# Ten adaLN pieces summed on VectorE and closed with a column of ones, in a two-block diffusion kernel

## The chip, the cores and the metric

One core of one Trainium2 chip runs the whole program as one launch. The metric is device time in microseconds, from the start of an execution to its end; the number given is the median of several executions. The inputs and the output are fp32 in the chip's main memory.

## The reference, cut to what matters

Two blocks of two layers each work on 256 latent rows and 256 context rows of width 1024. Each layer has adaLN modulation: a condition vector `c` (for latent rows) and another, `c_ctx` (for context rows), go through silu and one wide matrix, and the result is cut into shift, scale and gate columns.

```python
mod_lat = (silu_c @ ada_w[i] + ada_b[i])[:, None, :]
mod_ctx = silu_cc @ ada_w[i] + ada_b[i]
...
m = jax.nn.silu(cond) @ w_mod + b_mod
return jnp.split(m[..., None, :], N_MOD, axis=-1)
...
    if not last:
        hcf = modulate(rms_norm(xc, norm_ffn[l]), csh2, csc2)
        xc = xc + cg2 * conv_ffn(hcf, w_up[l], conv_w[l], w_down[l])
```

In the last layer of each block the context rows need only the first shift and scale (their keys and values are still read); the gate, and in the second block the second shift, scale and gate, are used for latent rows alone. The first block's matrices are 1024 x 3072, the second block's 1024 x 6144.

## The kernel before, in words

All weights arrive by DMA as raw fp32 chunks of 128 partitions x 1024 (512 KB). ScalarE casts a chunk to a high half in the matmul's reduced type (`whi`, L180 through the recording helper), VectorE subtracts it from the raw chunk for the low half (`wlo`), and each product is made of three matmuls: high by high, high by low, low by high (`mm3`, L195 at the matmul call). A unit of the feed-forward's up-projection is one chunk and 24 matmuls of 512 columns; it is called v or g and a number (v9, g10) after the table of orders. A down-projection unit is d and a number.

Three raw buffers (`RAW`, L97) and four pairs of high and low halves (`HL`) form a ring. `weights_hi` (L347) and `weights_lo` (L363) walk over all chunks in the order of use, one after the other; a chunk that may not be prepared yet holds up all behind it. `load_chunks` (L330) issues the next load on SyncE's queue when VectorE has subtracted a chunk. `run_items` (L392) takes the units in order and issues their matmuls. Other work (evictions, norms, the scan heads, the closing steps of adaLN pieces) runs as chains that are stepped by a clock of estimates while the program is written, so that one program order comes out for each engine.

The strings `L0_ORDER` (L148), `MIX1`, `MIX2` and `FFN` (L163) give the order of units by hand; each letter A is one adaLN chunk, taken from the list `ada_left` (L717 to L722). A piece is 512 columns of an adaLN matrix, four chunks of 256 rows x 512 columns: `mod1` has pieces 0 to 5, `bmod1` pieces 0 to 11. `ada_one` (L526) makes a piece as follows: the four columns of `cond` (silu of the two condition vectors, each as high and low part, tile `condc`) are the stationary side, a chunk's halves the moving side, 16 matmuls in all into a 4 x 512 bank; then ScalarE copies the bank to `ada_r`, TensorE transposes it in four parts, ScalarE copies that to `ada_t`, and VectorE adds the parts and the bias into the tile `mod1` or `bmod1`.

In the scan layer the pieces 4 and 5 of `mod1` stand as `z7 A q8 f8 A b8 A v8 A z8 A q9 f9 A b9 A z9 A o2 o3 q10 f10 A` (the first of these is the last chunk of piece 3). In the feed-forward of the second block's first layer the pieces 4 to 10 of `bmod1` stand between v8 and d8; after v8, v9, v11 and v12 come the last chunk of one piece and the first of the next, after v10 the last two and the first, after d4 the last chunk of piece 9 and two of piece 10. The four chunks of piece 11 stand alone in the last layer.

Of the kernel before, what the change touches and what calls it, by code (L numbers as in the profile page):

```python
# [20 lines left out]
P = 128  # L21
# [60 lines left out]
def tile_two_blocks(ctx: ExitStack, tc: tile.TileContext, I, out: bass.AP):  # L82
# [19 lines left out]
    def bank(kind="mm"):  # L102
        p = ps_mm if kind == "mm" else ps_sm
        return p.tile([P, 512], F32, tag="ps" + kind, name="ps" + kind)
# [7 lines left out]
    def small(tag, n=16):  # L112
        return sp.tile([P, n], F32, tag=tag, name=tag)
# [91 lines left out]
    def spawn(gen, delay=0.0):  # L205

        chains.append([when(*delay) if isinstance(delay, tuple) else clk[0] + delay, gen, None])

    def tell(key, t=None):

        done[key] = last[0] if t is None else t
# [288 lines left out]

    cst, mod = {}, {}

    def cond_split(cname, ccname):

        st = const.tile([P, KD, 4], F32R, tag="cond" + cname, name="cond" + cname)
        for j, nm in enumerate((cname, ccname)):
            sg = small("cs_s", 8)
            act.activation(sg[:, :8], col[nm], AF.Sigmoid)
            dve.tensor_tensor(sg[:, :8], sg[:, :8], col[nm], ALU.mult)
            act.copy(st[:, :, 2 * j], sg[:, :8])  # L510
            dve.tensor_tensor(st[:, :, 2 * j + 1], sg[:, :8], st[:, :, 2 * j], ALU.subtract)
        cst[cname] = st
# [10 lines left out]

    ada_open = {}

    def ada_one(w, cname, bias, b0, mname, j, k2):  # L526
        if (mname, j) not in ada_open:
            ada_open[mname, j] = []
        hold = ada_open[mname, j]

        def fin():
            r = sp.tile([4, 512], F32, tag="ada_r", name="ada_r", bufs=1)
            act.copy(r, hold[0][:4, :])
            sm_hold(-1)
            yield
            ps = bank("sm")
            for b in range(4):
                tr(ps[:, 4 * b:4 * b + 4], r[:, b * P:(b + 1) * P], ident[:4, :4])
            t4 = sp.tile([P, 16], F32, tag="ada_t", name="ada_t", bufs=2)
            act.copy(t4, ps[:, :16])  # L540
            v = t4.rearrange("p (b v h) -> p b v h", b=4, v=2)
            m = mod[mname][:, 4 * j:4 * j + 4, :]
            dve.tensor_tensor(m, v[:, :, :, 0], v[:, :, :, 1], ALU.add)
            dve.tensor_tensor(m, m, col[bias][:, b0 + 4 * j:b0 + 4 * j + 4].unsqueeze(2).to_broadcast([P, 4, 2]),
                              ALU.add)
            tell((mname, j))

        def run(wk):
            if k2 == 0:
                yield sm_room(1)  # L550
                sm_hold(1)
                hold.append(bank("sm"))
            for i in range(2):
                k = 2 * k2 + i
                mm(hold[0][:4, :], cst[cname][:, k, :], wk[i][0], k == 0, False)
                mm(hold[0][:4, :], cst[cname][:, k, :], wk[i][1], False, k == KD - 1)
            if k2 == 3:
                spawn(fin())
            yield 0

        return Item(run, cut(w[k2 * 256:(k2 + 1) * 256, j * 512:(j + 1) * 512]))
# [17 lines left out]
        tell("g" + name)  # L579


    def mod_cols(gain, m, sc, sh, name):

        A = const.tile([P, 8, 2], F32, tag="A" + name, name="A" + name)
        dve.tensor_scalar(A, m[:, sc:sc + 8, :], 1.0, None, ALU.add)
        dve.tensor_tensor(A, A, gain.unsqueeze(2).to_broadcast([P, 8, 2]), ALU.mult)
        return A, m[:, sh:sh + 8, :]


# [212 lines left out]
    def hgrn(hd):  # L802

        l0 = st.l0
        x, qs = st.X[hd], st.q[hd]
        Kd = l0.tile([P, T], F32, tag="Km", name="Kd", bufs=2)
        dve.tensor_tensor(Kd, x[:, 0], x[:, 3], ALU.add)
# [17 lines left out]
        for lv in range(7):  # L825
            h = 1 << lv
            nb = T // (2 * h)
            ps = bank("sm")
            for c in range(4):
                mm(ps[:, c * P:(c + 1) * P], Km[:, c * P:(c + 1) * P],  # L830
                   ap_of(x, T + c * P, [[2 * h, P // (2 * h)], [T + h, 2], [1, h]]), True, True)
            t = Tl.rearrange("p d (b s) -> p d b s", s=2)
            xs = x.rearrange("p k (b s i) -> p k b s i", s=2, i=h)
            dve.tensor_tensor(xs[:, 2:4, :, 1], xs[:, 2:4, :, 1],
                              t[:, :, :, 0].unsqueeze(3).to_broadcast([P, 2, nb, h]), ALU.mult)
            dve.tensor_tensor(xs[:, 0:2, :, 0], xs[:, 0:2, :, 0],
                              t[:, :, :, 1].unsqueeze(3).to_broadcast([P, 2, nb, h]), ALU.mult)
            Tl = l0.tile([P, 2, max(nb, 8)], F32, tag=f"T{lv + 1}", name="Tn", bufs=1)[:, :, :nb]
            dve.tensor_tensor(Tl, t[:, :, :, 0], t[:, :, :, 1], ALU.mult)
            dve.copy_predicated(A.rearrange("p c t -> p (c t)"),  # L840
                                st.lvl[:, lv].rearrange("p c t -> p (c t)"), ps)
            if lv < 6:
                yield (x,)
                Km = mixed_keys(lv + 1)
            yield (x, Km)
        if hd:
            yield has(("O", hd - 1))
        ps = bank("sm")
# [156 lines left out]
    def l1_kv_chain():  # L1005
        l1 = st.l1
        kv_r = st.kv_r
        ss, rs = small("pn_ss", 4), small("pn_rs", 4)
        jk = bank("sm")
        for tk in range(4):  # L1010
            act.activation(jk[:, tk * P:(tk + 1) * P], kv_r[:, tk, 0:128], AF.Square, accum_out=ss[:, tk:tk + 1])
        rsqrt(rs[:, 0:4], ss[:, 0:4], 1.0 / 128, 4)
        dve.tensor_tensor(kv_r[:, :, 0:128], kv_r[:, :, 0:128],
                          rs[:, 0:4].unsqueeze(2).to_broadcast([P, 4, 128]), ALU.mult)
        kp = row2k("kp", (P, 4, 1, 2, 64))
        for tk in range(4):
            src = kv_r[:, tk, 128:192].unsqueeze(1)
            if tk < 2:
                for j in range(2):
                    dve.tensor_copy(kp[:, tk, :, j], src)  # L1020
            else:
                rope_mla(kp[:, tk], src, tk - 2, 1)
        yield
        ps = bank("sm")
        for tk in range(4):
            tr(ps[:, tk * P:(tk + 1) * P], kv_r[:, tk, 0:128], ident)
        tm = row2k("tm")
        dve.tensor_scalar(tm, ps, col["kvan"], None, ALU.mult)
        split(st.kvT[0], st.kvT[1], tm)
        ps = bank("sm")  # L1030
        for tk in range(4):
            tr(ps[:, tk * P:(tk + 1) * P], kp[:, tk].rearrange("p a b c -> p (a b c)"), ident)

        kh = row2k("kh", dt=F32R)
        act.copy(kh, ps)
        dve.tensor_copy(st.kst[0:64], kh[0:64])
        dve.tensor_tensor(st.kst[64:128], ps[64:128], kh[64:128], ALU.subtract)
        tm = row2k("tm2", (P, 4, 128))
        dve.tensor_tensor(tm, kv_r[:, :, 0:128], st.kvg.unsqueeze(1).to_broadcast([P, 4, 128]), ALU.mult)
        split(st.kvR[0], st.kvR[1], tm)  # L1040
        tell("kv")

    def l1_qa_chain():
        qa_r = st.qa_r
        ss, rs = small("pn_ss", 4), small("pn_rs", 4)
        jk = bank("sm")
        for tk in range(2):
            act.activation(jk[:, :256], qa_r[:, tk], AF.Square, accum_out=ss[:, tk:tk + 1])
        rsqrt(rs[:, 0:2], ss[:, 0:2], 1.0 / 256, 2)
        dve.tensor_tensor(qa_r, qa_r, rs[:, 0:2].unsqueeze(2).to_broadcast([P, 2, 256]), ALU.mult)  # L1050
        yield
        ps = bank("sm")
        for k in range(2):
            for tk in range(2):
                tr(ps[:, k * 256 + tk * P:k * 256 + (tk + 1) * P], qa_r[:, tk, k * P:(k + 1) * P], ident)
        tm = row2k("tm", (P, 2, 256))
        for k in range(2):
            dve.tensor_scalar(tm[:, k], ps[:, k * 256:(k + 1) * 256], col["qan"][:, k:k + 1], None, ALU.mult)
        split(st.qaT[0], st.qaT[1], tm)
        tell("qa")  # L1060
# [273 lines left out]
    def b2_items(l):  # L1334
# [378 lines left out]
        def ffn_norm(g):  # L1713
            yield mods(bm, 24, 40)
            if l not in st.ABf:
                st.ABf[l] = mod_cols(col["ffn"][:, 8 * l:8 * l + 8], mod[bm], 32, 24, f"f{l}")
            yield from norm_chain([xr[tk] for tk in g], lambda: st.ABf[l], 1 - g[0] // 2, hT[fk], g, fkey, ())


# [170 lines left out]
    for i in range(2):  # L1890
        for _ in load_cols(i):
            pass
    cond_split("c", "cc")
    for nm in ("mod0", "mod1"):
        mod[nm] = const.tile([P, 24, 2], F32, tag=nm, name=nm)
# [130 lines left out]
```

## Time and profile before

| | |
|---|---|
| median of 3 runs | 2336.43 us (2333.97 to 2337.26) |
| the profiled execution, its own time | 2340.02 us |
| its span, first to last instruction | 2338.0 us |
| granted TensorE clock, mean | 0.983 |
| busy: TensorE, VectorE, ScalarE | 96%, 71%, 48% of the span |
| chain that ended last | TensorE 85%, VectorE 7%, ScalarE 2%, DMA 2% |

The profile is one execution. Busy is the time in which an engine had an instruction under way; a matmul's time in it includes its way through the array, so the distance between two starts tells how long the queue is held. An idle stretch in front of an instruction is put down to what ended it.

### The profile page before, as it was taken

What the parts mean: (1) busy time and instruction counts of PE and PEld (TensorE: products, weight loads), DVE (VectorE), ACT (ScalarE), POOL (GpSimd) and SP (SyncE); (2) the same over time, 40 slices, a digit from 0 to 9 for tenths busy, and PEclk for the clock granted to TensorE, in tenths of its full rate; (3) what the DMA queues carried; (4) which work ended last, traced back from release to release, by engine and by line L of the source; (5) the groups of instructions that cost most, each with busy time, mean ns of one, the idle gap of its engine ahead of it and who ended that gap; (6) DMA issues with size and microseconds to landing.
All of it is one profiled execution on the core that took longest, in us unless ns stands there. A gap on an engine that the chain in (4) does not pass through costs nothing.

```text
span 2338.0 us, 33916 instructions
## 1 busy us (share of the span) xinstructions
PE 2237.4 (96%) x13051; PEld 1903.2 (81%) x13051; DVE 1669.5 (71%) x3016; ACT 1124.7 (48%) x1963; POOL 35.8 (2%) x38
## 2 busy tenths in 40 slices
PE   5999999999999987999899999999999999998998
PEld 3888888888888877888788878877777888997987
DVE  6677867777778777888657844688746646876976
ACT  7344444444444445556445533556523335655644
POOL 0000000000000000000000000100010010000000
PEclk8999999999999998999999999999999999999999
DMA  7223324332434233233422344277643233455664
GB/s 253 68 73 116 101 91 126 91 108 91 131 96 126 91 107 94 77 110 113 146 82 91 90 146 124 63 216 210 210 141 109 90 109 112 134 171 154 190 189 135
DMA packets 324042, 290.63 MB, mean 124 GB/s; under 512 B 10561, under 2 KB 257705, under 8 KB 323881
## 3 DMA queue, kind: packets, MB, share of 16 engines
q1 hardware_dynamic: 323881, 288.47, 40.4%
q8 instruction: 103, 1.69, 0.3%
q14 instruction: 58, 0.48, 0.1%
HBM read 287.34 MB, written 1.09 MB: 123 GB/s over the span
## 4 chain that ended last, share of the span: by engine, by line
PE 85%; DVE 7%; ACT 2%; DMA 2%; issue 1%; SPq 0%; DVEq 0%; ACTq 0%
PE psmm L195 63%; PE pssm L195 18%; PE pssm L201 3%; DVE wlo L180 2%; ACT whi L180 1%; DMA wraw<-in_w_in_dram 1%; DMA wraw<-in_w_mod_dram 0%; DVE x L180 0%; DMA wraw<-in_w_out_dram 0%; DVE rs_t L180 0%; ACT pssm L180 0%; DVE hlo L180 0%; DVE PT L180 0%; DVE nh_t L180 0%; DVE rp L180 0%
## 5 line engine op out<-in xcount | busy, mean ns | idle before, releaser
L180 DVE TENSOR_TENSOR wlo<-wraw,whi 128x1024 fp32r<-128x1024 f32 (+1 forms) x504 | 608.0, 1218 | 190.4 <-ACT whi L180 184.0
L180 ACT CAST whi<-wraw 128x1024 fp32r<-128x1024 f32 (+1 forms) x504 | 519.0, 1039 | 392.5 <-PE psmm L195 276.9
L195 PE MATMUL psmm<-hhi,whi 128*128 128x512 f32 (+1 forms) x1832 | 654.5, 357 | 5.1 <-ACT hhi L180 2.8
L195 PE MATMUL psmm<-hhi,wlo 128*128 128x512 f32 (+1 forms) x1832 | 637.6, 348 | 13.4 <-DVE wlo L180 13.4
L195 PE MATMUL psmm<-hlo,whi 128*128 128x512 f32 (+1 forms) x1832 | 636.4, 347 | 4.8 <-DVE hlo L180 4.8
L195 PEld LDWEIGHTS psmm<-hhi,wlo 128*128 128x128 f32 x1832 | 352.0, 192 | 58.6 <-DVE wlo L180 15.5
L195 PEld LDWEIGHTS psmm<-hhi,whi 128*128 128x128 f32 x1832 | 352.8, 193 | 48.9 <-ACT whi L180 3.1
L195 PEld LDWEIGHTS psmm<-hlo,whi 128*128 128x128 f32 x1832 | 352.7, 193 | 42.5 <-DVE hlo L180 5.8
L180 DVE TENSOR_TENSOR X<-X,Tn 128x512 f32<-128x512 f32 x192 | 124.0, 688 | 56.5 <-PE pssm L195 28.9
L195 PE MATMUL psmm<-whi,yh 128*128 128x512 f32 x412 | 163.7, 397 | 0.4 <-ACT yh L180 0.4
L195 PE MATMUL psmm<-wlo,yh 128*128 128x512 f32 x412 | 160.7, 390 | 0.4 <-DVE wlo L180 0.4
L195 PE MATMUL psmm<-whi,yl 128*128 128x512 f32 x412 | 160.7, 390 | 0.0
L195 PE MATMUL psmm<-whi,hhi 128*128 128x256 f32 x464 | 136.6, 294 | 1.8 <-ACT hhi L180 1.7
L195 PE MATMUL psmm<-wlo,hhi 128*128 128x256 f32 x464 | 132.8, 286 | 5.4 <-DVE wlo L180 5.3
L195 PE MATMUL psmm<-whi,hlo 128*128 128x256 f32 x464 | 133.0, 287 | 0.9 <-DVE hlo L180 0.9
L195 PE MATMUL pssm<-X,Km 128*128 128x128 f32 x896 | 126.7, 285 | 1.3 <-ACT Km L180 1.3
L180 ACT COPY Km<-X 128x512 f32<-128x512 f32 x112 | 74.5, 666 | 108.1 <-DVE X L180 73.3
L195 PEld LDWEIGHTS pssm<-X,Km 128*128 128x128 f32 x896 | 119.8, 191 | 7.8 <-ACT Km L180 2.1
L180 DVE SCALAR_TENSOR_TENSOR conv<-psmm,cols,conv 128x510 f32<-128x510 f32 (+1 forms) x176 | 107.9, 614 | 25.3 <-ACT conv L180 22.2
L195 PE MATMUL pssm<-whi,condc 128*4 128x512 f32 x256 | 102.2, 399 | 0.0
L195 PE MATMUL pssm<-wlo,condc 128*4 128x512 f32 x256 | 101.1, 395 | 0.0
L195 PEld LDWEIGHTS psmm<-wlo,hhi 128*128 128x128 f32 x464 | 89.9, 194 | 7.0 <-DVE wlo L180 6.3
(350 smaller groups left out, 3317.3 us busy)
## 6 DMA issues: line engine op xcount, KB each, us to landing
wraw<-in_w_mod_dram SPq DMA_DIRECT2D x96, 512.0 KB
wraw<-in_w_up_dram SPq DMA_DIRECT2D x88, 512.0 KB
wraw<-in_hg_w_in_dram SPq DMA_DIRECT2D x80, 512.0 KB
wraw<-in_w_in_dram SPq DMA_DIRECT2D x68, 512.0 KB
wraw<-in_w_down_dram SPq DMA_DIRECT2D x40, 512.0 KB
wraw<-in_ada_w_dram SPq DMA_DIRECT2D x32, 512.0 KB
wraw<-in_mla_w_in_dram SPq DMA_DIRECT2D x20, 512.0 KB
sraw<-in_ada_w_dram SPq DMA_DIRECT2D x16, 512.0 KB
```

The source lines that it names most:

```text
L180: r = fn(*a, **k)
L195: pe.matmul(o, a, b, start=start, stop=stop)
L201: pe.transpose(o, i, idn)
```

## The change

For ten pieces (`mod1` 4 and 5, `bmod1` 4 to 11) `ada_one` hands over to the new `ada_lat`. A piece is a running sum `ada_s` of 128 x 512: ScalarE scales the first row tile of the piece by its silu column, VectorE adds the other seven row tiles, each raw tile times its column, in one multiply-add. Then four matmuls with the sum as weights and a column of ones as the moving side add over partitions, and VectorE adds the bias into the latent column only. There is one accumulator buffer, with the tag that `ada_r` has; a piece's first chunk waits for the close of the piece ahead (`ada_after`). A chunk of such a piece has no high and low half and no matmul of its own. Two more things move: a head of the scan layer starts after the levels of the head ahead, and some small tiles share a tag.

```diff
@@ cond_split
+    cfull = {}
+
...
-            sg = small("cs_s", 8)
+            sg = cfull[cname] if j == 0 else small("cs_s", 8)
@@ ahead of ada_one
+    ada_prev = [None, {}]
+
+    def ada_after(key):
+        if key not in ada_prev[1]:
+            ada_prev[1][key] = has(*ada_prev[0] or ())
+            ada_prev[0] = (key,)
+        return ada_prev[1][key]
+
+    def latent_only(mname, j):
+
+        return (mname, j) in (("mod1", 4), ("mod1", 5)) or mname == "bmod1" and j >= 4
+
+    def ada_lat(w, cname, bias, b0, mname, j, k2):
+        key = (mname, j)
+        free = ada_after(key)
+
+        def hi(raw):
+            if k2 == 0:
+                ada_open[key] = sp.tile([P, 512], F32, tag="ada_r", name="ada_s", bufs=1)
+                act.activation(ada_open[key], raw[:, :512], AF.Copy, scale=cfull[cname][:, 0:1])
+            return ada_open[key]
+
+        def lo(raw, acc):
+            for i in range(2):
+                k = 2 * k2 + i
+                if k:
+                    dve.scalar_tensor_tensor(acc, raw[:, i * 512:(i + 1) * 512], cfull[cname][:, k:k + 1], acc,
+                                             ALU.mult, ALU.add)
+            return [acc]
+
+        def fin(acc):
+            ps = bank("sm")
+            for b in range(4):
+                mm(ps[:, b:b + 1], acc[:, b * P:(b + 1) * P], st.one[:, 0:1], True, True)
+            c = b0 + 4 * j
+            dve.tensor_tensor(mod[mname][:, 4 * j:4 * j + 4, 0], ps[:, 0:4], col[bias][:, c:c + 4], ALU.add)
+            tell(key)
+            yield
+
+        def run(wk):
+            if k2 == 3:
+                spawn(fin(wk[0]), (wk[0],))
+            yield 0
+
+        rows = w[k2 * 256:(k2 + 1) * 256, j * 512:(j + 1) * 512]
+        return Item(run, [([rows], (hi, lo), free if k2 == 0 else None)])
@@ ada_one
+        if latent_only(mname, j):
+            return ada_lat(w, cname, bias, b0, mname, j, k2)
+        free = ada_after((mname, j))
...
         def fin():
-            r = sp.tile([4, 512], F32, tag="ada_r", name="ada_r", bufs=1)
+            yield free
+            r = sp.tile([P, 512], F32, tag="ada_r", name="ada_r", bufs=1)[:4, :]
@@ hgrn
+        if hd:
+            yield has(("lvl", hd - 1))
...
+        tell(("lvl", hd), 0.0)
@@ l1_kv_chain and l1_qa_chain
-        ss, rs = small("pn_ss", 4), small("pn_rs", 4)
+        ss, rs = small("hg_ss", 4), small("hg_rs", 4)
@@ ffn_norm (mod_cols takes nv columns of the table)
-                st.ABf[l] = mod_cols(col["ffn"][:, 8 * l:8 * l + 8], mod[bm], 32, 24, f"f{l}")
+                st.ABf[l] = mod_cols(col["ffn"][:, 8 * l:8 * l + 8], mod[bm], 32, 24, f"f{l}", 1 if last else 2)
```

On TensorE, in the feed-forward stage between unit v10 and unit g10 (bank `psmm_15321`), where piece 5 of `bmod1` ends (bank `pssm_15184`) and piece 6 begins; before the change (three more such rows stand ahead):

```order
L195 MATMUL pssm_15184<-wlo_15231,condc2_905 4x512
L195 MATMUL pssm_15184<-whi_15247,condc2_905 4x512 [waits Activation_49]
L195 MATMUL pssm_15184<-wlo_15263,condc2_905 4x512 [waits DVE_49]
L195 MATMUL pssm_15184<-whi_15247,condc2_905 4x512
L195 MATMUL pssm_15184<-wlo_15263,condc2_905 4x512
L195 MATMUL pssm_15315<-whi_15258,condc2_905 4x512 [waits Activation_49]
L195 MATMUL pssm_15315<-wlo_15273,condc2_905 4x512 [waits DVE_49]
L195 MATMUL pssm_15315<-whi_15258,condc2_905 4x512
L195 MATMUL pssm_15315<-wlo_15273,condc2_905 4x512
L195 MATMUL psmm_15321<-hhi_13802,whi_15292 128x512 [waits Activation_49]
L195 MATMUL psmm_15321<-hlo_13803,whi_15292 128x512
L195 MATMUL psmm_15321<-hhi_13802,wlo_15305 128x512 [waits DVE_49]
```

and with the change, from the close of piece 5 (the accumulator `ada_s_15091`) to the first matmuls of g10:

```order
L195 MATMUL pssm_15180<-one_123,ada_s_15091 128x1 [waits DVE_49]
L195 MATMUL pssm_15180<-one_123,ada_s_15091 128x1 x3
L195 MATMUL psmm_15210<-hhi_13744,whi_15193 128x512 [waits PE_49,Activation_49]
L195 MATMUL psmm_15210<-hlo_13745,whi_15193 128x512
L195 MATMUL psmm_15210<-hhi_13744,wlo_15201 128x512 [waits DVE_49]
```

Twelve narrow matmuls between the two units became four of one column.

On ScalarE at the same place before: `conv_15298` is the eviction of v10, `whi_15292` the cast for g10.

```order
L180 CAST whi_15258<-wraw_15218 128x1024 [waits DMAHW5_49,DVE_49,PE_49]
L180 ACTIVATE fsg_15270<-conv_15245 128x512 [waits DVE_49,Activation_49]
L180 CAST whi_15292<-wraw_15233 128x1024 [waits DMAHW6_49,PE_49]
L180 ACTIVATE conv_15298<-psmm_15249,cols3_840 128x512 [waits PE_49]
L180 CAST yh_15284<-conv_15177 128x512 [waits DVE_49]
```

With the change the eviction of v10 is `conv_15189`, the scaled copy that opens piece 6 is `ada_s_15191`, and the cast for g10 is `whi_15193`:

```order
L180 ACTIVATE conv_15144<-psmm_15109,cols3_841 128x512 [waits PE_49]
L180 ACTIVATE fsg_15174<-conv_15144 128x512 [waits DVE_49,Activation_49]
L180 ACTIVATE conv_15189<-psmm_15150,cols3_841 128x512 [waits PE_49]
L180 ACTIVATE ada_s_15191<-wraw_15135,cfc2_106 128x512 [waits DMAHW5_49,PE_49]
L180 CAST whi_15193<-wraw_15139 128x1024 [waits DMAHW6_49]
```

The cast for g10 stood ahead of v10's eviction and stands now behind it and behind the scaled copy, which waits for TensorE.

On VectorE at this place with the change: `bmod1` is the bias add of piece 5, `conv_15189` the eviction of v10, `wlo_15201` the low half for g10.

```order
L180 TENSOR_TENSOR bmod1_120<-pssm_15180,cols2_806 128x4 [waits PE_49]
L180 TENSOR_TENSOR conv_15089<-conv_15089,fsg_15174 128x512 [waits DVE_49,Activation_49]
L180 SCALAR_TENSOR_TENSOR conv_15189<-psmm_15150,cols3_841,conv_15189 128x2x255 [waits Activation_49]
L180 SCALAR_TENSOR_TENSOR conv_15189<-psmm_15150,cols4_869,conv_15189 128x2x255 [waits DVE_49]
L180 SCALAR_TENSOR_TENSOR ada_s_15191<-wraw_15135,cfc2_106,ada_s_15191 128x512 [waits DMAHW5_49,Activation_49]
L180 TENSOR_TENSOR wlo_15201<-wraw_15139,whi_15193 128x1024 [waits DMAHW6_49,Activation_49]
```

The low half for g10 comes behind the bias add, a product, the eviction of v10 and the first multiply-add of piece 6.

## Rows read from the trace of the kernel before

**Rows 1.** The page's part 1: busy time, share of the span and instructions by engine.

```profile
PE 2237.4 (96%) x13051; PEld 1903.2 (81%) x13051; DVE 1669.5 (71%) x3016; ACT 1124.7 (48%) x1963; POOL 35.8 (2%) x38
```

**Rows 2.** Busy time by stretch: length, PE, PEld, DVE, ACT, POOL, clock, DMA.

```profile
300.00:600.00 300.00, 300.00 (x1772) 254.27 (x1771) 221.72 (x395) 131.33 (x225) 0.00 (x0) 1.00 0.34 102
...
1600.00:1740.00 140.00, 139.57 (x626) 99.46 (x625) 97.86 (x119) 71.96 (x94) 6.50 (x4) 1.00 0.65 199
```

**Rows 3.** Groups by line: count, busy us and mean ns, idle before.

```profile
L195 PE MATMUL pssm<-whi,condc 128*4 128x512 f32 x256 | 102.2, 399 | 0.0
```

**Rows 4.** Timeline of TensorE, feed-forward stage: start us, duration, engine, line, operation.

```profile
1598.77 0.40 PE L195 MATMUL pssm<-whi,condc 128*4 128x512 f32 x1
1599.00 0.40 PE L195 MATMUL pssm<-wlo,condc 128*4 128x512 f32 x1
...
1601.32 0.40 PE L195 MATMUL psmm<-hhi,whi 128*128 128x512 f32 x1
1601.55 0.39 PE L195 MATMUL psmm<-hlo,whi 128*128 128x512 f32 x1
...
1602.11 0.41 PE L201 MATMUL pssm<-ident,ada_r 4*128 4x4 f32 x4
```

**Rows 5.** Timeline of TensorE in the scan layer: four fp32 matmuls (eight records).

```profile
320.75 1.05 PE L195 MATMUL pssm<-X,Km 128*128 128x128 f32 x8
321.56 0.48 PE L195 MATMUL psmm<-whi,yh 128*128 128x512 f32 x1
```

**Rows 6.** Timeline of TensorE: first adaLN matmul behind v8, v9, v10, v11, v12, d4.

```profile
1613.99 0.40 PE L195 MATMUL pssm<-whi,condc 128*4 128x512 f32 x1
...
1629.21 0.40 PE L195 MATMUL pssm<-whi,condc 128*4 128x512 f32 x1
...
1643.48 0.40 PE L195 MATMUL pssm<-whi,condc 128*4 128x512 f32 x1
...
1659.58 0.40 PE L195 MATMUL pssm<-whi,condc 128*4 128x512 f32 x1
...
1674.80 0.40 PE L195 MATMUL pssm<-whi,condc 128*4 128x512 f32 x1
...
1716.10 0.40 PE L195 MATMUL pssm<-whi,condc 128*4 128x512 f32 x1
```

**Rows 7.** Timeline of ScalarE, feed-forward stage, with the idle time before and its end.

```profile
1598.97 0.69 ACT L180 ACTIVATE conv<-psmm,cols 128x512 f32<-128x512 f32 x1 [0.94 <-PE psmm L195]
1599.56 1.04 ACT L180 CAST whi<-wraw 128x1024 fp32r<-128x1024 f32 x1
...
1603.58 1.05 ACT L180 CAST whi<-wraw 128x1024 fp32r<-128x1024 f32 x1 [0.61 <-DMA wraw<-in_w_up_dram]
```

**Rows 8.** Timeline of VectorE, feed-forward stage.

```profile
1599.69 1.53 DVE L180 SCALAR_TENSOR_TENSOR conv<-psmm,cols,conv 128x510 f32<-128x510 f32 x2 [0.50 <-ACT conv L180]
1601.14 1.22 DVE L180 TENSOR_TENSOR wlo<-wraw,whi 128x1024 fp32r<-128x1024 f32 x1
```

**Rows 9.** Two DMA issues on SyncE, and a stretch after the lone one.

```profile
1598.62 0.37 SPq L188 DMA_DIRECT2D wraw<-in_w_up_dram  x1
...
314.69 0.37 SPq L188 DMA_DIRECT2D wraw<-in_hg_w_in_dram  x1
...
318.00:318.50 0.50, 0.50 (x4) 0.39 (x3) 0.50 (x2) 0.00 (x0) 0.00 (x0) 1.00 0.01 2
```

**Rows 10.** TensorE around an idle stretch (timeline), and busy time and clock behind it.

```profile
1757.96 0.50 PE L195 MATMUL psmm<-hhi,wlo 128*128 128x512 f32 x1 [2.19 <-DVE wlo L180]
...
1758.00:1759.00 1.00, 1.00 (x4) 0.86 (x5) 1.00 (x2) 0.00 (x0) 0.00 (x0) 0.89 0.01 3
1759.00:1762.00 3.00, 3.00 (x8) 2.33 (x8) 1.18 (x2) 0.00 (x0) 0.00 (x0) 0.50 0.83 242
1762.00:1763.00 1.00, 1.00 (x5) 0.77 (x5) 0.00 (x0) 0.71 (x1) 0.00 (x0) 0.90 1.01 294
```

**Rows 11.** Busy time by stretch in the last layer, around an adaLN chunk.

```profile
2205.00:2210.00 5.00, 5.00 (x41) 4.49 (x39) 4.54 (x10) 3.06 (x6) 0.00 (x0) 1.00 0.58 157
```

More of the change, by code (lines that the diff above doesn't have):

```diff
@@ L579, in gate_rows, with mod_cols @@
         tell("g" + name)
-    def mod_cols(gain, m, sc, sh, name):
+    def mod_cols(gain, m, sc, sh, name, nv=2):
         A = const.tile([P, 8, 2], F32, tag="A" + name, name="A" + name)
-        dve.tensor_scalar(A, m[:, sc:sc + 8, :], 1.0, None, ALU.add)
-        dve.tensor_tensor(A, A, gain.unsqueeze(2).to_broadcast([P, 8, 2]), ALU.mult)
+        dve.tensor_scalar(A[:, :, :nv], m[:, sc:sc + 8, :nv], 1.0, None, ALU.add)
+        dve.tensor_tensor(A[:, :, :nv], A[:, :, :nv], gain.unsqueeze(2).to_broadcast([P, 8, nv]), ALU.mult)
         return A, m[:, sh:sh + 8, :]
@@ L1044, in l1_qa_chain @@
         qa_r = st.qa_r
-        ss, rs = small("pn_ss", 4), small("pn_rs", 4)
+        ss, rs = small("hg_ss", 4), small("hg_rs", 4)
         jk = bank("sm")
@@ L1892, in tile_two_blocks @@
             pass
+    cfull["c"], cfull["c2"] = (const.tile([P, 32], F32, tag="cf" + nm, name="cf" + nm)[:, :8] for nm in ("c", "c2"))
     cond_split("c", "cc")
```

## The prediction

> **What bounds the kernel now.** I read the page's busy times first: TensorE is busy 2237 of 2338 us [rows 1]. Then the busy times by stretch: in the first block's scan layer TensorE is busy 300.0 of 300 us, and in the feed-forward stage around 1600 to 1740 us it is busy 139.57 of 140, while VectorE is busy 97.86 there [rows 2]. So in both places where most of the changed pieces stand, time is TensorE's queue: a matmul taken out shortens the kernel, and a wait put into that queue lengthens it.
>
> **What the change takes from TensorE.** Of the old way the trace has 256 narrow matmuls over high halves, 8 a piece [rows 3], and as many over low halves: 16 a piece, in 4 chunks of two row tiles. Their mean of 399 ns is latency; they start every 0.23 us (1598.77 to 1599.00), a piece closes with four small transposes of 0.41 us together, and the wide matmuls around them start every 0.23 us too (1601.32, 1601.55) [rows 4]. One old piece is 16 x 0.23 + 0.41 = 4.1 us. A new piece has four plain fp32 matmuls of one column by 128x128 weights. No row shows that shape; the nearest are four fp32 matmuls of 128 columns, which hold the queue from 320.75 to 321.56, 0.81 us [rows 5]. Below stand the four transposes, 0.41. The column width is small in both, the weight loads are those of rows 5, so I take 0.85. Gain 3.25 us a piece, 32 us for ten, if nothing else happened.
>
> **ScalarE and VectorE.** ScalarE drops four casts of 1.05 us a piece and gains one scaled copy of some 0.6 [rows 7]: nothing on the path by itself. VectorE drops four subtractions of 1.22 and gains seven dependent multiply-adds of 512. Two such operations of 510, the second waiting for the first, take 1.53 [rows 8], so seven cost 5.3 us against 4.9: no change, and covered while VectorE has 42 us idle in 140 [rows 2].
>
> **Scan layer (two pieces).** Both `mod1` pieces end two whole units ahead of the next piece's first chunk, so the new wait of that chunk is over before TensorE comes to the weights behind it. TensorE is always busy there: the gain is 2 x 3.25 = 6.5 us. The new rule that a head's scan starts after the levels of the head ahead moves rows, not work; I cost it at nothing because TensorE has projection matmuls to run meanwhile; if that cover failed at one head the price would be one wait as in rows 10, 4 us with its slow stretch. Ends: -6.5 and -2.5.
>
> **Last layer (one piece).** Its chunks stand alone among narrow units; around the last one TensorE is busy 5.00 of 5.00 us [rows 11]. At most 3.25; the row covers one chunk of the four, so I take 2.5. Ends -3.25 and 0. The halved column table and the renamed small tiles: nothing.
>
> **Feed-forward of the first layer (seven pieces): the gain meets a new wait.** The accumulator is a single buffer. So a piece's first chunk may be scaled by ScalarE only after TensorE has read the previous piece's sum, and the order shows ScalarE's cast of the next unit's weights behind that scaled copy, where before it stood ahead of the eviction. Five such boundaries come with a unit directly behind (after v8, v9, v10, v11, v12) and one with a down-projection unit (after d4). Count from the slot behind the last matmul of the unit ahead, for instance 1598.77.
>
> - TensorE: column matmuls from 0 to 0.85.
> - ScalarE: eviction from 0.20 (1598.97), the next start 0.59 later [rows 7]; scaled copy 1.1 (0.25 for the way of the wait) to 1.65; cast of the next weights to 2.7. TensorE's first two matmuls run at 2.75 to 3.2.
> - VectorE, in its order: bias add (waits for the column matmuls) to 1.2, a product to 1.8, two eviction operations to 3.25, the multiply-add of the new piece to 3.95, the low half of the next weights to 5.15 [rows 8]. TensorE's third matmul goes at 5.2, and the other 21 behind it end at 10.2.
>
> Without the wait that unit would end at 0.85 + 5.45 = 6.3: a boundary costs 3.9 us where the piece gave 3.25. Then two more prices.
>
> **The clock.** TensorE idled 2.19 us ahead of 1757.96, and the granted clock then read 0.89, 0.50 and 0.90 of full over five microseconds: 0.11 + 1.5 + 0.1 = 1.7 us of work lost at the lower level, 1.2 GHz [rows 10]. Each boundary has two idle stretches of 1.9 and 2.0 us; part of the slow time falls into the second one, so I take 1.2 a boundary, ends 0 and 2.5. The Trainium skill, TensorE: Matmul & The Clock Gate, section on oscillation, says that a loop whose matmuls wait in every turn drops to half clock in every turn and pays the change each time. By that rule the price is the full 1.7 at all six boundaries, 3 us more, and the sum below would be +5.7, 2342: just on the slower side. The one case of rows 10 agrees; no row here shows a series of them.
>
> **The raw ring.** Three raw buffers; a load goes out when VectorE has finished with a buffer, and a load issued at 1598.62 ended a wait at 1603.58, 5.0 us [rows 7, 9]; a lone one issued at 314.69 had its data in by 318.0, 3.3 us [rows 9]. Where two chunks of a piece lie between the boundary's unit and the next, the next unit's load goes out at 5.15, lands at 10.15, is cast by 11.2 and has its low half by 12.4: that unit ends at 12.45 + 5.0 = 17.45. After v9 only one chunk lies between, the load goes at 3.95, and TensorE is the later one: 10.2 + 1.2 + 5.45 = 16.9. After v8 the old piece's four matmuls and its copy, transposes and second copy come ahead of the scaled copy; the same count gives the third matmul at 5.5 and 17.8.
>
> The same stretches before run from 1613.99 to 1629.21, 1643.48, 1659.58 and 1674.80, and to 1716.10 at d4's end [rows 6]: 15.2, 14.3, 16.1, 15.2 and 41.3 us. After: 17.8, 16.9, 17.45, 17.45, and from v12 to d4's end 17.7 for g12 and d0, 0.85, and four units of 5.45 without a wait (d1 lies between pieces): 40.35. Differences +2.6, +2.6, +1.35, +2.2, -0.95. After d4, d5's low half comes behind three multiply-adds, at 4.6; d6's load goes out at 3.9, lands at 8.9 and has its low half at 11, so d6 ends at 16.3, with the clock 16.7. Before, three chunks, transposes, d5, a chunk and d6 were 2.76 + 0.41 + 2.73 + 0.92 + 5.45 = 12.3: +4.4. The last piece gives 0.5. Sum **+11.7 us**; with no loss of clock and loads of 3.3 us it is +2, with 2.5 us of clock +17.
>
> **Sum.** -6.5 - 2.5 + 11.7 = +2.7 us on the profiled execution's 2340.0; it ran 3.6 us above the median of the three runs, 2336.4, so the same sum gives **2339 us**, a change of 0.1%. A measurement of this kernel can tell about 0.2%, 4.7 us, from no change. Forecast: no difference that can be told, 2332 to 2341.
>
> **Rivals.**
>
> 1. *The gain comes through.* If ScalarE and VectorE reached the next unit's weights before TensorE finished the unit ahead, the boundaries would cost nothing: 2336.4 - 32 = 2304. For it: TensorE idles 0.4 us of 140 now, so the supply has kept up [rows 2]. Against: the cast stands behind the scaled copy in one in-order queue, and that copy waits for TensorE. Between it and the forecast lie boundaries without a loss of clock and with quick loads: -6.5 - 3.25 + 2 = -8, 2328. Together 0.27.
> 2. *Slower: the half clock at each boundary.* If every boundary's slow stretch outlasts both idle stretches, 2.5 us are lost at six places: +17 - 6.5 - 2.5 = +8, 2344; with the scan layer's gain cut to 2.5 as well, 2348. It decides from about 1.5 us a boundary on, where the sum passes +4.7. 0.35.
> 3. *VectorE becomes the bound in the feed-forward.* It would need 15 us for two units and a piece; evictions, products and low halves of two units are 2 x 1.53 + 2 x 0.7 + 0.7 + 2 x 1.22 and the piece 5.3: 13 us. Close, and it would end near rival 2. 0.03 of its 0.35.
> 4. *The pieces aren't changed.* The order has ten closing copies fewer and ten groups of column matmuls; excluded.
>
> **Numbers.** Forecast 0.38, rival 1 0.27, rivals 2 and 3 0.35. The range reaches from 2327, where boundaries are cheap, to 2347, where the clock is lost; it leaves out the full gain and the worst of the slow cases. Faster by over 0.2%: 0.27; within: 0.38; slower: 0.35.
>
> **What would show it.** Right: the page has 160 rows of the narrow matmuls fewer on TensorE; the waits on TensorE in the feed-forward stretch grow from under 3 us to 20 to 30, put down to ScalarE's cast and to VectorE's low half, in pairs of about 2 us every 16 to 17 us; the clock there falls below 0.95; the scan layer is about 6 us shorter. Wrong: no new waits in that stretch and a span some 30 us shorter (rival 1), or two matmuls' starts staying 0.23 us apart right behind the waits, so that the clock costs nothing. If the scan layer does not get shorter, the new order rule of the heads took the gain.

## The result, and the profile after

The changed kernel takes 2349.1 us (median of four runs, 2347.2 to 2354.8) against 2336.1 for the kernel before in the same comparison: ratio 1.0063, 95% interval 1.0051 to 1.0076. It is slower by 0.6%, 13 us, and lies above the forecast (2332 to 2341) and above the range (to 2347). The profiled execution of the changed kernel was the fastest of its four (2347.17), and that of the kernel before took 2340.02 us, longer than any of its four, so the two profiles differ by 7 us only. The page's part 1 and the busy time by stretch of the changed kernel:

```profile
PE 2215.5 (94%) x12931; PEld 1901.0 (81%) x12931; DVE 1671.2 (71%) x3036; ACT 1086.5 (46%) x1913; POOL 35.7 (2%) x38
```

```profile
300.00:600.00 300.00, 300.00 (x1793) 259.02 (x1792) 222.44 (x403) 126.28 (x225) 0.00 (x0) 1.00 0.35 106
1600.00:1740.00 140.00, 117.12 (x472) 91.06 (x471) 93.36 (x124) 39.79 (x53) 6.45 (x4) 0.89 0.56 176
```

TensorE is busy 22 us less than before [rows 1] and the kernel is longer. In the middle of the scan layer TensorE is still busy throughout. Between 1600 and 1740 us it idles 22.9 us where it idled 0.4, and the clock is 0.89 [rows 2]. The waits of TensorE in that stretch (what was waited for; us in total, times, longest):

```profile
PE psmm L195 <- DVE wlo L180: 12.0, 8, 2.8
PE psmm L195 <- ACT whi L180: 10.1, 6, 1.8
```

They come in pairs. The boundary after v9, TensorE's timeline:

```profile
1629.79 0.39 PE L195 MATMUL psmm<-hhi,wlo 128*128 128x512 f32 x1
1630.02 0.95 PE L195 MATMUL pssm<-one,ada_s 128*128 128x1 f32 x8
1632.71 0.50 PE L195 MATMUL psmm<-hhi,whi 128*128 128x512 f32 x1 [1.75 <-ACT whi L180]
1633.05 0.40 PE L195 MATMUL psmm<-hlo,whi 128*128 128x512 f32 x1
1635.06 0.77 PE L195 MATMUL psmm<-hhi,wlo 128*128 128x512 f32 x1 [1.61 <-DVE wlo L180]
1635.63 0.63 PE L195 MATMUL psmm<-hhi,whi 128*128 128x512 f32 x1
1636.06 0.63 PE L195 MATMUL psmm<-hlo,whi 128*128 128x512 f32 x1
```

ScalarE over the same boundary:

```profile
1630.22 0.69 ACT L180 ACTIVATE conv<-psmm,cols 128x512 f32<-128x512 f32 x1 [0.31 <-PE psmm L195]
1631.01 0.72 ACT L180 ACTIVATE ada_s<-wraw,cfc 128x512 f32<-128x512 f32 x1
1631.63 1.03 ACT L180 CAST whi<-wraw 128x1024 fp32r<-128x1024 f32 x1
```

VectorE over the same boundary:

```profile
1631.01 0.16 DVE L180 TENSOR_TENSOR bmod<-pssm,cols 128x4 f32<-128x4 f32 x1 [1.75 <-PE pssm L195]
1631.08 0.68 DVE L180 TENSOR_TENSOR yl<-conv,yh 128x512 fp32r<-128x512 f32 x1
1631.68 1.53 DVE L180 SCALAR_TENSOR_TENSOR conv<-psmm,cols,conv 128x510 f32<-128x510 f32 x2
1633.13 0.74 DVE L180 SCALAR_TENSOR_TENSOR ada_s<-wraw,cfc,ada_s 128x512 f32<-128x512 f32 x1
1633.79 1.22 DVE L180 TENSOR_TENSOR wlo<-wraw,whi 128x1024 fp32r<-128x1024 f32 x1
```

This is the prediction's count, operation by operation: the cast stands behind the scaled copy, the low half behind the new piece's multiply-add. TensorE's third matmul goes 5.04 us behind the slot (predicted 5.2). Then matmuls start 0.43 us apart, not 0.23. Busy time and clock behind the pair (columns as in [rows 2]):

```profile
1633.00:1635.00 2.00, 0.45 (x2) 0.01 (x1) 2.00 (x4) 0.00 (x0) 0.00 (x0) 1.00 0.01 3
1635.00:1637.00 2.00, 1.94 (x5) 1.56 (x6) 1.42 (x3) 0.00 (x0) 0.00 (x0) 0.53 0.94 270
1637.00:1639.00 2.00, 2.00 (x7) 1.59 (x6) 0.21 (x1) 1.04 (x1) 0.00 (x0) 0.62 0.85 290
```

That is (0.47 + 0.38) x 2 = 1.7 us lost to the lower level, 1.2 GHz, as much as in [rows 10].

### The profile page after: what moved, and what is told of

Same layout as the page of the kernel before. It is cut to its first block, busy times and chain, and to the rows that moved or that the text cites. A ratio compares the mean times of both kernels' runs of the same rounds, so it can differ in the third digit from the quotient of the medians.

```text
span 2345.1 us, 33578 instructions
## 1 busy us (share of the span) xinstructions
PE 2215.5 (94%) x12931; PEld 1901.0 (81%) x12931; DVE 1671.2 (71%) x3036; ACT 1086.5 (46%) x1913; POOL 35.7 (2%) x38
## 4 chain that ended last, share of the span: by engine, by line
PE 84%; DVE 7%; ACT 2%; DMA 1%; issue 1%; DVEq 0%; SPq 0%; ACTq 0%
PE psmm L195 64%; PE pssm L195 18%; PE pssm L201 3%; DVE wlo L180 2%; ACT whi L180 1%; DMA wraw<-in_w_out_dram 1%; DVE x L180 1%; ACT pssm L180 0%; DVE rs_t L180 0%; DVE hlo L180 0%; DVE nh_t L180 0%; DMA wraw<-in_w_in_dram 0%; DVE ada_s L180 0%; DVE PT L180 0%; DVE rt L180 0%
## 5 line engine op out<-in xcount | busy, mean ns | idle before, releaser
L180 DVE TENSOR_TENSOR wlo<-wraw,whi 128x1024 fp32r<-128x1024 f32 (+1 forms) x464 | 558.7, 1216 | 181.1 <-ACT whi L180 174.4
L180 ACT CAST whi<-wraw 128x1024 fp32r<-128x1024 f32 (+1 forms) x464 | 476.9, 1039 | 396.8 <-PE psmm L195 246.2
L195 PEld LDWEIGHTS psmm<-wlo,yh 128*128 128x128 f32 x412 | 77.9, 189 | 20.2 <-DVE wlo L180 5.6
L195 PEld LDWEIGHTS psmm<-whi,yh 128*128 128x128 f32 x412 | 78.0, 189 | 17.8 <-ACT whi L180 2.2
```

The source lines that it names most:

```text
L180: r = fn(*a, **k)
L195: pe.matmul(o, a, b, start=start, stop=stop)
```

## The experiments

All ratios are to the kernel before on the same chip, with their 95% intervals. "FF" is the feed-forward stage of the second block's first layer in the run's profile, from the matmul that ends the wait near 1493 us to the one that ends the wait near 1758 us (times of the kernel before). In the profile of the kernel before it is 265.0 us; in the seven other profiles with the old pieces in this stage it is 262.8 to 263.5 us, and the last section says where the 2 us come from.

| run | what it is | median us | ratio | FF us |
|---|---|---|---|---|
| the change | | 2349.1 | 1.0063 (1.0051 to 1.0076) | 279.0 |
| e_rule_only | all but the pieces | 2340.8 | 1.0024 (1.0014 to 1.0034) | 263.3 |
| e_lvl | before, with the rule of the heads | 2340.4 | 1.0017 (1.0008 to 1.0026) | 263.0 |
| e_rest | all but the pieces and the rule | 2335.2 | 0.9998 (0.9990 to 1.0007) | 263.0 |
| e_scan_only | rule and the two mod1 pieces | 2334.0 | 0.9994 (0.9985 to 1.0003) | 263.0 |
| e_two_acc | the change, two accumulators | 2323.0 | 0.9946 (0.9934 to 0.9959) | 251.0 |
| e_shift | the change, chunks moved | 2332.2 | 0.9983 (0.9974 to 0.9992) | 261.2 |
| e_copy_dve | the change, first copy on VectorE | 2352.7 | 1.0070 (1.0057 to 1.0082) | 282.8 |
| e_raw4 | the change, fourth raw buffer | 2345.8 | 1.0042 (1.0029 to 1.0054) | 275.5 |
| e_before_raw4 | before, fourth raw buffer | 2335.8 | 0.9999 (0.9990 to 1.0008) | 262.8 |
| e_gates | the change, gates side by side | 2350.4 | 1.0064 (1.0051 to 1.0076) | 280.4 |
| e_two_gates | two accumulators, gates | 2321.4 | 0.9944 (0.9932 to 0.9957) | 253.7 |
| e_two_gates_raw4 | the same, fourth raw buffer | 2315.1 | 0.9913 (0.9900 to 0.9927) | 246.5 |
| e_lvl_from3 | before, rule from head 3 on | 2337.3 | 1.0015 (1.0006 to 1.0024) | 263.1 |
| e_lvl_mid | before, rule for heads 3 to 13 | 2334.6 | 0.9997 (0.9988 to 1.0006) | 263.5 |
| e_best_mid | two accumulators, fourth raw buffer, rule for heads 3 to 13 | 2309.7 | 0.9891 (0.9878 to 0.9905) | 245.1 |

### The scan layer: pieces or rule?

The first theory was that the boundary waits cost the feed-forward stage its 14 us and that the rule of the heads ate the two `mod1` pieces' gain. Two runs split the change.

e_rule_only (`latent_only` returns `False`):

> All twelve-row pieces go the old way over TensorE; of the change only the rest is left: a head's scan starts after the levels of the head ahead, the renamed small tiles, the halved column table, the wait of a piece's eviction for the piece ahead. Theory A (the rule of the heads moves the second gate transposition three row groups later, and TensorE then waits some 6 us for the last row tiles of the scan layer): slower than before by 4 to 7 us, about 2341 us, with an idle stretch of about 6 us on TensorE between 860 and 880 us. Rival B (the rule costs nothing and the two mod1 pieces themselves give nothing in the scan layer): 2336 us, the same as before within 0.1%.

e_scan_only (`latent_only` returns `(mname, j) in (("mod1", 4), ("mod1", 5))`):

> Only the two mod1 pieces of the scan layer go the new way, the ten pieces' other eight the old way. Theory A (the two pieces do give 3.25 us each, the rule of the heads takes it): 6.5 us below the run in which only the rule is left, so the same as before, 2334 to 2337 us; the first gate transposition stands about 5 us earlier than in that run. Rival B (the pieces give nothing in the scan layer, the rule costs nothing): the same time as that run. Either way the feed-forward stage has no new waits: 265 us as before.

Theory A holds in both: with the rule 0.24% slower, with the two pieces added back to 0.9994. The pieces give 0.30%, 7.0 us for two; the prediction had 6.5. (Each ratio is known to 0.1%, 2.3 us.) Then the rule was run by itself, and its counterpart.

e_lvl:

```
+        if hd:
+            yield has(("lvl", hd - 1))
...
+        tell(("lvl", hd), 0.0)
```

> The kernel before, with nothing of the change but the rule that a head's scan starts after the levels of the head ahead. Theory A (the rule alone costs the scan layer its 5 to 6 us, partly by waits at the first heads near 180 us and the rest at the layer's end): 2341 us, idle stretches of about 1 us near 177 and 180 us and of 6 us near 873 us. Rival B (the other leftovers, the waits between pieces' evictions and the renamed tiles, cost it): 2336 us, and the run with those alone costs it.

e_rest (e_rule_only without those two waiting lines):

> The counterpart: all pieces the old way, the other leftovers of the change (evictions of pieces one after the other, renamed small tiles, the halved column table), but not the rule of the heads. Theory A: the same as before within 0.1%, 2334 to 2337 us. Rival B: 2340 to 2342 us.

The rule alone makes the kernel slower; the other leftovers make no difference that can be told. Where it costs, in e_lvl's timeline of TensorE:

```profile
177.26 0.63 PE L201 MATMUL pssm<-ident,on 128*128 128x128 f32 x4 [1.02 <-DVE on L180]
178.41 0.41 PE L201 MATMUL pssm<-ident,ada_r 4*128 4x4 f32 x4 [0.52 <-ACT ada_r L180]
180.45 0.50 PE L195 MATMUL psmm<-hhi,wlo 128*128 128x512 f32 x1 [0.98 <-DVE wlo L180]
...
873.37 3.76 PE L201 MATMUL pssm<-ident,xn 128*128 128x128 f32 x16 [6.12 <-DVE xn L180]
```

and in its busy times, where the clock reads 0.66 behind the first three:

```profile
180.00:184.00 4.00, 3.55 (x10) 2.83 (x11) 3.31 (x5) 1.21 (x3) 0.00 (x0) 0.66 0.45 131
```

The kernel before, at the same two places:

```profile
174.81 1.16 PE L195 MATMUL pssm<-X,Km 128*128 128x128 f32 x8 [0.79 <-ACT Km L180]
...
865.08 2.16 PE L201 MATMUL pssm<-ident,xn 128*128 128x128 f32 x16 [1.51 <-DVE xn L180]
868.49 0.38 PE L195 MATMUL psmm<-whi,hhi 128*128 128x256 f32 x1 [1.25 <-ACT hhi L180]
870.97 0.38 PE L195 MATMUL psmm<-wlo,hhi 128*128 128x256 f32 x1 [2.10 <-DVE wlo L180]
```

For the end of the layer I had a theory of the place: the second gate's transposition stands at 846.0 us in the changed kernel and at 840.5 before, so the gate arrives late. e_gates makes both side by side:

```
-                yield from gate_rows(gt[:, v], ...)
+                spawn(gate_rows(gt[:, v], ...))
+            yield has("gate00", "gate01")
```

> As the change, but the two gate rows of the first layer are made side by side, so that the second gate's transposition stands directly behind the first on TensorE and not three row groups later. Theory A (the rule of the heads costs 5 us because that transposition, and with it the gate's way through DRAM, comes late): the idle stretch of 6.1 us near 867 us shrinks to 1 to 2 us, some 5 us less than the change: 2343 to 2345 us. Rival B (the rule costs because the last head's scan itself ends later): the idle stretch stays within 1 us of 6.1 and the time at 2349 us.

The theory fell. VectorE's gate products begin at 850.7 instead of 853.8 us, and TensorE's idle stretch before the transposes is 5.87 us:

```profile
865.81 2.48 PE L201 MATMUL pssm<-ident,xn 128*128 128x128 f32 x10 [5.87 <-DVE xn L180]
```

In the changed kernel it is 6.11 us. So the late gate is not what ends that wait. Two more runs gave the rule to a part of the heads only.

e_lvl_from3 (`if hd > 2:` in e_lvl):

> The kernel before with the rule of the heads alone, but only from the fourth head on. Theory A (of the rule's 4 to 5 us some 3 are the idle stretches near 177 to 180 us, where the first heads' scans stand one after the other, and the half clock behind them; the rest is at the layer's end): the stretches near 177 to 180 us go back to 0.8 us at full clock, the 6.1 us near 870 us stay, 2337 to 2338 us. Rival B (all of it is at the layer's end): 2340 us.

e_lvl_mid (`if 3 <= hd <= 13:`):

> The same with the rule from the fourth to the fourteenth head only, so that the last two heads may run side by side again. Theory A (the end's part comes from the last heads, whose scans stand one after the other): no idle stretch beyond those of the kernel before, 2335 to 2336.5 us. Rival B (the end's part comes from the middle of the layer, where the rule has shifted the order once and for all): the idle stretch of 6.1 us near 870 us stays, 2337 to 2338 us.

From the idle stretch that ends at 152 us to the second transposes near 885 us, the profiles give 732.9 us before, 740.2 in e_lvl, 736.8 in e_lvl_from3 and 733.6 in e_lvl_mid: some 3.5 us at the first heads, 3 at the last two. With the rule off for the first heads the stretches of 177 to 180 us are gone and the 6.1 us remain; with it off for the last two heads as well, these are gone too. e_lvl_from3, then e_lvl_mid:

```profile
870.51 3.77 PE L201 MATMUL pssm<-ident,xn 128*128 128x128 f32 x16 [6.12 <-DVE xn L180]
```

```profile
863.17 2.16 PE L201 MATMUL pssm<-ident,xn 128*128 128x128 f32 x16 [1.51 <-DVE xn L180]
```

The first heads' part rests on the profiles: the ratios of e_lvl and e_lvl_from3, 1.0017 and 1.0015, don't tell it apart. e_lvl_mid is as fast as the kernel before. One thing stays open: in this stretch the rule costs 7.3 us by the profiles (740.3 in e_rule_only too), and 4 to 5.6 by the ratios. Which step of the last heads' scans comes late was not followed further.

### The boundaries of the feed-forward stage

e_two_acc (pieces of the second block alternate between two tiles):

```
+        if mname == "bmod1":
+            free = has((mname, j - 2))
...
-                ada_open[key] = sp.tile([P, 512], F32, tag="ada_r", name="ada_s", bufs=1)
+                ada_open[key] = (row2k("ada_s") if mname == "bmod1" and j % 2 == 0 else
+                                 sp.tile([P, 512], F32, tag="ada_r", name="ada_s", bufs=1))
```

> As the change, but the pieces of the second block alternate between two accumulators, and a piece's first scaled copy waits for the piece before last. Theory A (the wait of the single accumulator makes the boundary): the six pairs of idle stretches go, the seven pieces give their 3.25 us, and the feed-forward stage lasts about 265 - 23 = 242 us instead of 279; the kernel about 2349 - 37 = 2312 us. Rival B (the three raw buffers and VectorE's low halves set the pace; the accumulator only shows it first): the waits for VectorE's low half stay, at most the first idle stretch of each boundary goes (six times 1.75 us), 2338 to 2342 us. Rival C (VectorE becomes the bound with its seven dependent multiply-adds a piece): a unit pair with a piece takes about 13 to 15 us of VectorE, 2320 to 2330 us, TensorE waiting for low halves all along.

The pairs are gone and the stage is 28 us shorter than with one accumulator: the new wait is what made the stage slow. But 251 is not the expected 242. Two units and a piece take 13.8 us (column matmuls at 1653.17, 1666.94 and 1680.83) where TensorE has 11.7 of work, and what is left are small waits for low halves. One unit of e_two_acc on TensorE, on ScalarE and on SyncE:

```profile
1648.04 0.50 PE L195 MATMUL psmm<-hhi,wlo 128*128 128x512 f32 x1 [0.42 <-DVE wlo L180]
```

```profile
1645.67 1.05 ACT L180 CAST whi<-wraw 128x1024 fp32r<-128x1024 f32 x1 [4.76 <-DMA wraw<-in_w_up_dram]
```

```profile
1641.82 0.37 SPq L188 DMA_DIRECT2D wraw<-in_w_up_dram  x1
```

The load goes out at 1641.82, when VectorE has freed a buffer, and the cast waits for it until 1645.67. The time is in rival C's range; that the load buffers, and not VectorE, set most of what is left is shown by the run with a fourth one, below. e_shift keeps the single accumulator and moves three chunks (one from behind v8 to behind d0, two from behind d4 to behind d5 and d6), so that a whole unit lies at each boundary:

```
-v8 A A g8 A A v9 A A g9 A v10 ... d0 A d1 A d2 A d3 A d4 A A A d5 A d6 d7 A d8
+v8 A g8 A A v9 A A g9 A v10 ... d0 A A d1 A d2 A d3 A d4 A d5 A A d6 A d7 A d8
```

> As the change, with its single accumulator, but in the feed-forward stage's order one chunk is moved so that at each of the six boundaries a whole unit of matmuls lies between the last chunk of a piece and the first chunk of the next. Theory A (what costs is that the cast of the next unit's weights stands behind the waiting scaled copy): the cast now stands ahead of it, the sum is read before the scaled copy's turn, the idle pairs go, and the time is near that of the run with two accumulators, 2312 to 2320 us. Rival B (raw buffers or VectorE set the pace): waits move to other units, 2338 to 2349 us.

The order of the queues alone takes back 18 us of the stage (279.0 to 261.2), with no memory. It stays 10 us behind two accumulators, between the two theories: waits remain, the longest where two chunks now stand ahead of d6:

```profile
1718.30 0.80 PE L195 MATMUL psmm<-wlo,yh 128*128 128x512 f32 x1 [4.74 <-DVE wlo L180]
```

e_copy_dve takes the scaled copy off ScalarE:

```
-                act.activation(ada_open[key], raw[:, :512], AF.Copy, scale=cfull[cname][:, 0:1])
...
+                if k == 0:
+                    dve.tensor_scalar(acc, raw[:, :512], cfull[cname][:, 0:1], None, ALU.mult)
```

> As the change, with its single accumulator, but a piece's first scaled copy is done by VectorE ahead of its first multiply-add, so that nothing on ScalarE waits for TensorE's reading of the sum. Theory A (of the two idle stretches at a boundary the first, 1.75 us, is ScalarE's cast behind that copy, the second, 1.61 us, VectorE's low half behind the first multiply-add): the first stretch goes, the second stays or grows by up to 1 us, a boundary costs about 1.5 to 2.5 us less: 2349 - 6 x 2 = 2337 us, 2334 to 2341. Rival B (the low half sets the end of the boundary in any case): the first stretch goes, the second grows by as much, 2347 to 2350 us.

Rival B: nothing is won. TensorE in e_copy_dve, at one boundary:

```profile
1667.94 0.95 PE L195 MATMUL pssm<-one,ada_s 128*128 128x1 f32 x8
1669.81 0.50 PE L195 MATMUL psmm<-hhi,whi 128*128 128x512 f32 x1 [0.93 <-ACT whi L180]
...
1673.49 0.79 PE L195 MATMUL psmm<-hhi,wlo 128*128 128x512 f32 x1 [2.95 <-DVE wlo L180]
```

The first stretch falls from 1.75 to 0.93 us and the second grows from 1.61 to 2.95: VectorE's low half, behind the new piece's first two products in its own queue, sets the end. So it takes both queues to be clear of the new piece, which e_shift does and moving one operation does not.

e_raw4 and e_before_raw4 (the changed kernel and the kernel before with a fourth buffer for raw weights, in that stage's memory):

> The change with its single accumulator and a fourth raw buffer in the feed-forward stage. The prediction's step had the boundary's end at 17.45 us by the load that goes out late, and 16.9 us where TensorE is the later one. Theory A (that step: the raw ring adds about 0.5 us at three boundaries and up to 3 us after d4, the accumulator's wait the rest): 2 to 5 us less than the change, 2344 to 2347 us, and the idle pairs of 1.75 and 1.61 us stay. Rival B (the ring is most of the boundary): the pairs shrink to under 1 us each and the time falls by more than 8 us, below 2341 us.

> The kernel before with the same fourth raw buffer, as a control for what the buffer gives without the change. Theory A (TensorE idles only 0.4 of 140 us there, so an earlier load has nothing to end): the same as before within 0.1%, 2334 to 2337 us. Rival B (the buffer helps whatever the pieces are): some 6 us less, 2330 us.

Theory A in both. With one accumulator the buffer gives 3.5 us of the stage and the pairs stay, as at e_raw4's boundary after v10; the kernel before gains nothing from it.

```profile
1648.07 0.50 PE L195 MATMUL psmm<-hhi,whi 128*128 128x512 f32 x1 [1.75 <-ACT whi L180]
1650.41 0.70 PE L195 MATMUL psmm<-hhi,wlo 128*128 128x512 f32 x1 [1.61 <-DVE wlo L180]
```

Then the mends together.

e_two_gates:

> Two accumulators and the side-by-side gates together. If the two costs are separate, as theory A has it, the gains add: 2323 - 5 = 2318 us. If they overlap (a later stage takes up the time), 2321 to 2324 us.

As e_gates gives nothing, nothing adds: 0.9944 against 0.9946 for e_two_acc, 2321.4 us.

e_two_gates_raw4:

> As the run before it, with a fourth raw buffer during the feed-forward stage, out of that stage's own memory. Theory A (with the accumulator's wait gone, the pace of 13.8 us for two units and a piece, where TensorE has 11.7 us of work, is set by the three raw buffers: the cast waits 4 us for a load that went out late): TensorE's waits there go to under 3 us, the stage lasts 251 - 8 = 243 us, the kernel 8 us less than the run before it. Rival B (VectorE, busy 49 of 56 us there, sets the pace): VectorE's low half stays the one that is waited for, and the stage gets at most 3 us shorter.

6.3 us less by the medians, nearer to theory A's 8 than to rival B's 3: the three buffers were most of what was left. Behind them VectorE comes close to being the bound, 50.97 of 56 us; its busy times in that stretch:

```profile
1624.00:1680.00 56.00, 53.06 (x249) 42.98 (x248) 50.97 (x73) 23.58 (x31) 0.00 (x0) 1.00 0.76 240
```

e_best_mid (two accumulators, fourth buffer, rule for heads 3 to 13):

> All ten pieces the new way with two accumulators in the second block, the fourth raw buffer in the feed-forward stage, and the rule of the heads from the fourth to the fourteenth head only. If the rule's cost goes with its ends, as theory A has it, 2315 - 4 = 2311 us; if it does not (rival B), 2313 to 2316 us.

2309.7 us, 1.1% faster than the kernel before: with the rule confined to the middle heads the scan layer's gain comes through as well. The first gate transposition (of `g_c`) comes at 828.4 us against 836.0 before, and the stretch from 152 us to the second transposes lasts 725.8 us, against 732.3 in e_two_gates_raw4.

## Why the prediction was wrong, step by step

- **The step that failed: "I cost it at nothing because TensorE has projection matmuls to run meanwhile".** By the ratios the rule of the heads costs 4 to 5.6 us (e_lvl, e_rule_only), at the first heads and at the last two, where TensorE then waits: the cover fails there. The prediction had priced a failure at 4 us "at one head" and chosen 0. Its last sentence named the sign, a scan layer that does not get shorter, and that is what the profile shows: the feed-forward stage begins at 1492.9 us against 1493.0.
- **The `mod1` pieces** gave 7.0 us (predicted 6.5). Where the next matmul does not wait, four column matmuls hold the queue for 0.81 us, as in [rows 5] (0.85 taken). In the scan layer of the changed kernel:

```profile
475.48 0.95 PE L195 MATMUL pssm<-one,ada_s 128*128 128x1 f32 x8
476.29 0.47 PE L195 MATMUL psmm<-hhi,whi 128*128 128x512 f32 x1
```

- **Last layer.** From the end of FF to the end of the span the change takes 573.2 us, and the kernel before 580.0. But this stretch varies more from profile to profile than the piece can give: 575.3 to 580.0 us in the eight profiles with the old piece 11, 573.2 to 577.8 in the nine with the new one. By the means, 577.0 and 575.6, it is -1.4 (predicted -2.5), and no run tells it from nothing.
- **Feed-forward.** The mechanism was right, and so was nearly every interval: 17.4, 17.2, 17.5, 17.5 and 41.1 us (predicted 17.8, 16.9, 17.45, 17.45, 40.35). But the stage is 16.0 us longer than e_scan_only's, against +11.7. **Most of the missing part is after d4:** from there to the stage's end 48.6 us, predicted 45.8. The load went out and landed as counted, but VectorE, in order, had two multiply-adds and two gate products ahead of d6's low half, and GpSimd ran its adds of the residual beside them. VectorE's timeline, then GpSimd's (POOL), then TensorE's:

```profile
1731.18 2.48 DVE L180 SCALAR_TENSOR_TENSOR ada_s<-wraw,cfc,ada_s 128x512 f32<-128x512 f32 x2
1733.58 1.27 DVE L180 TENSOR_TENSOR rt<-psmm,gc 128x512 f32<-128x512 f32 x2
1734.78 3.59 DVE L180 TENSOR_TENSOR wlo<-wraw,whi 128x1024 fp32r<-128x1024 f32 x2
```

```profile
1730.13 2.98 POOL L180 TENSOR_TENSOR x<-x,rt 128x512 f32<-128x512 f32 x2 [259.79 <-DVE rt L180]
1734.34 3.49 POOL L180 TENSOR_TENSOR x<-x,rt 128x512 f32<-128x512 f32 x2 [1.23 <-DVE rt L180]
```

```profile
1736.74 0.49 PE L195 MATMUL psmm<-wlo,yh 128*128 128x512 f32 x1 [2.79 <-DVE wlo L180]
```

  TensorE goes on 13.4 us behind d4, not 11. The prediction counted neither the queue nor the company: beside GpSimd's adds the two multiply-adds take 2.48 us, 1.53 elsewhere, and d6's low half, the first of the two in its row, 1.90 instead of 1.22. These two make 1.6 of the 2.4 us, by an estimate from these rows; no run moves GpSimd's adds. The kernel before shows the same: a low half of 512 columns takes 1.47 us beside them (1722.61) and 0.69 elsewhere.
- **The clock.** Taken 1.2 us a boundary. In the changed kernel's stage 56 starts of wide matmuls stand about 0.43 us apart and not 0.23: 11 us in all, against 7.2. The half clock came at six boundaries of six, 9.4 us (1.0 to 2.4 each), and once more behind the wait of d6, 1.6 us. The Trainium skill, TensorE: Matmul & The Clock Gate, section on HAM oscillation, has the clock fall again in every turn of a loop that waits for its data; the trace agrees, six falls of six, though the waits of the page's loop are 3 to 5 us long and those here 0.5 to 2 us, in pairs. Behind v10 and v11 the next load sets the interval (17.5 us; 17.2 with the fourth buffer of e_raw4), and the slow stretch is covered by it, so that these intervals hardly grew.
- **The sum.** -7.0 + 5 - 1.4 + 16.0 = +12.6 us on the kernel before, against the measured 13; the prediction's was +2.7. Of the 10 us between the two sums 5 are the rule, 4.3 the feed-forward stage and 1.1 the last layer; the scan layer's pieces gave 0.5 more than predicted. Rival 2 had the right side, and the half clock at every boundary, but its +8 did not count the rule either, and its 2.5 us a boundary is more than the 1.0 to 2.4 measured.

## What to carry to other kernels

A buffer that is filled by one engine and read by another needed two copies here (28 us of the stage), or a unit of other work between the reading and the next filling (18 us). Behind a single one, ScalarE and VectorE each held back everything that was queued behind the waiting instruction, and clearing one of the two queues won nothing. Matmuls taken out of a full TensorE queue pay at their price only while the supply behind them keeps up; mend the waits in the order in which they appear (accumulator, then load buffers, then VectorE). A rule on order can be free in the middle of a layer and cost at its two ends; price it there, by the waits that the profile shows.

## What had not been expected of the hardware

- The same idle stretch does not always cost the clock. Behind the 2.08 us near 1493 us the clock read 0.50 in the kernel before, and 1.00 in the changed kernel behind 2.07 us, with the same matmuls on both sides. Of the 17 profiles of this case it fell there in three (the kernel before, e_two_gates, e_two_gates_raw4). In busy time by stretch, before and after:

```profile
1493.00:1495.00 2.00, 2.00 (x9) 2.00 (x10) 2.00 (x2) 0.00 (x0) 0.00 (x0) 0.50 0.36 99
```

```profile
1493.00:1495.00 2.00, 2.00 (x17) 2.00 (x18) 2.00 (x2) 0.00 (x0) 0.00 (x0) 1.00 0.44 121
```

  Such a fall is worth about 2 us: the stage behind it is 265.0 us in the kernel before and 262.8 to 263.5 in the seven profiles with the same pieces and no fall there. So a difference of a few us between two single profiles need not come from the change.
- Four fp32 matmuls of one column hold TensorE's queue as long as four of 128 columns, with weights of the same size: 0.81 us in both ([rows 5], and at 475.48 us in the changed kernel).
- VectorE's low halves and multiply-adds took longer in the rows where GpSimd added beside them: a low half of 128x1024 lasted 1.90 us at 1734.78 in the changed kernel, against 1.22.
